# Six weight subtractions on another engine, dt's rows in another buffer, and a scheduler that estimates matmuls and a shared port differently, in a two-layer recurrent decoder step

## The chip, the cores and the metric

One Trainium2 chip, one of its cores. The metric is the device time of one execution in microseconds. Engines as the profile names them: PE (matrix products), PEld (its weight loads), DVE and ACT (elementwise work, both can read PSUM), POOL (elementwise work on SBUF alone here), SP (issues most DMAs).

## What is computed

One step of a two-layer decoder trunk, for a prompt of 512 tokens and 8 samples of one token (520 columns in all), width 1024, all in float32.

```python
# layer 0
u = rmsnorm(h, norm_w) @ w_in
a_x, a_gate, b_z, b_xbc, b_dt = split(u)
a_xc = causal_conv(a_x, s_ac, a_conv_w, a_conv_b)
a_y, new_ah = rg_lru(a_xc, s_ah, a_w_r, a_b_r, a_w_i, a_b_i, a_lam)
a_out = a_y * silu(a_gate)
xbc = silu(causal_conv(b_xbc, s_bc, b_conv_w, b_conv_b))
dt = softplus(b_dt + b_dt_bias)
y, new_bs = ssd_scan(bx, dt, -exp(b_a_log), bb, bcm, s_bs)     # cumulative sums of dt * a by chunk
b_out = group_norm((y + b_d * bx) * silu(b_z)) * b_norm_w
h = h + concat(a_out, b_out) @ w_out
h = h + sigmoid(h @ ple_g) * (p @ ple_w)
# layer 1
q, fx, v, gate = split(rmsnorm(h, norm_w) @ w_in)
o, new_c = hgrn2_scan(q, k, v, g, s_c)                          # 16 heads, k and g from fx
h = h + (head_norm(o) * c_norm_w * silu(gate)) @ w_out
h = h + sigmoid(h @ ple_g) * (p @ ple_w)
# end
y = rmsnorm(h, norm_f)
```

## The kernel before

Every large matrix product is a block of 128 output features over all 520 columns, as two halves of 260. Products run in a reduced 32-bit form (fp32r), so a weight tile wraw that a 1 MB DMA brings is split into whi (a cast) and wlo (wraw - whi, a subtraction), and the tokens into xh and xl; a block of 1024 inputs is 3 x 8 x 2 = 48 matmuls: hi x hi, lo x hi, hi x lo. The splits are most of the work of DVE and ACT.

The stages follow each other on PE. First the transposes of the tokens and the embedding product pl of layer 0 (weights wraw7 and pp, evacuated through the tile htmp and stored to DRAM as pl_d). Then layer 0's projections: ax0 to ax7 (the RG-LRU branch; tokens normed to n and sqt, split to xnh and xnl; the first two blocks' weights are called wax), the gates g (weights gw, inputs xg), xbc (through the tile bcs; POOL keeps a copy of its sample columns in LCb), the SSD chunks (yd, with the decay matrix built in wsl), the gate and z projections, the output projection, the embedding gate. Layer 1 begins with pl of its own (evacuated by plt, stored to pl_d) while its norm is formed (n1b, acc1, n, xh), then f, q, v and g of 16 heads in pairs, with the small products A, kt, kv, o and ot of each head among them. The tail is the last norm.

dt's chain: dt_project (L1168) multiplies the tokens by dtws into two PSUM banks, copies them to a tile dth, and transposes dth into the bank dtT; DVE adds the bias, ACT takes exp, log1p_of (L920) on POOL evaluates a series of some twenty instructions on the tile dtt, and PE multiplies dtt by a triangle into acs, the cumulative sums that every SSD chunk needs.

dth has the tag "misc", and that tag has one buffer. The raw embedding input, each xg0 to xg7, and two tiles of the LRU's and the samples' outputs have the same tag. They take the buffer in the order in which the program names them.

What sets the order of the work. Helpers (tt, stt, ts, copy, ...) do not issue anything; they record operations (L269) with a priority, the place in the main stream of matrix products, shifted by the `side` that surrounds them. Plan.order (L348) then runs a list schedule over the engines with an estimate of every instruction: an engine that comes free takes the ready operation with the earliest priority. urgency (L336) puts what the main stream waits for ahead by MARGIN, unless its side is pinned. issue (L494) emits everything in this order, at one line of the file, L510. So all engines' queues are decided by the estimates. The estimate of a 260-column matmul is 260 columns at 2.4 per ns and 0.003 us on top (0.111 us), and double where the clock is thought halved. No estimate has DVE and POOL in each other's way.

```python
c = c + 0.003 * len(calls) if cols[int(t / 3.41333) - 1] >= 3060 else 2.0 * c
...
dth = new("cst", [2 * NH, D], "misc", "dth")
```

split_unit(u, hi, lo, eng) at L627 splits one weight tile: the cast on ACT or DVE (the planner's choice), the subtraction on eng.

Of the kernel before, what the change touches and what calls it, by code (L numbers as in the profile page):

```python
# [11 lines left out]
F32 = mybir.dt.float32  # L12
# [7 lines left out]
PSUM = bass.MemoryType.PSUM  # L20
# [7 lines left out]
D = 1024  # L28
# [11 lines left out]
SYNC = 0.12  # L40
PATIENCE = 3.26
ROW = 1 << 24
# how far ahead of a unit its weights are split and loaded, in us of the main stream
SPLIT_AHEAD, LOAD_AHEAD = 1.67, 11.54
# how far ahead of the main stream goes what it waits for, in us
MARGIN = 38.78
# an engine waits for an instruction that is more urgent by URGENT us, up to this part of the time of the one at hand
# [32 lines left out]
def _mm(n, a, k):  # L80
    out, m = k["out"] if "out" in k else a[0], k["lhsT"].shape[-1]
    if m < 128 and out.off >= 32 * ROW:
        # beside the one before it, in other columns of the array
        return 65 if k["rhs"].dtype == F32R else 125
    return max(n, 256) if k["rhs"].dtype == F32R else 4 * max(n, m)
# [16 lines left out]

class Buf:
    """A tile that is allocated when its first instruction is issued."""
# [7 lines left out]
class View:  # L112
    """A view of a Buf; offset and strides are in elements, a partition is ROW apart."""
# [86 lines left out]
class Op:  # L200
    """One instruction, in a form for each engine that may take it, or a few matrix products that stay together."""
# [8 lines left out]
class Plan:  # L210
    """Instructions are collected first and then put in an order: with an estimate of what each of them costs, an
    engine that comes free takes the instruction of the earliest place in the program whose operands are there."""
# [6 lines left out]
    # -- collecting --  # L219
# [23 lines left out]
    def side(self, start=0.0, rate=0.0, pinned=False):  # L243
        """Instructions whose place is moved, by a start and by their own time so far; pinned: for good."""
# [6 lines left out]
    def together(self, *views):  # L251
        """Instructions that wait until all of some operands are written."""
# [5 lines left out]
    def block(self, main=False):  # L258
        """Matrix products that stay together."""
# [66 lines left out]
    # -- ordering --  # L326
    def hold_banks(self):
        """A PSUM bank is taken only when what its readers wait for otherwise is already on its way."""
# [7 lines left out]
    def urgency(self):  # L336
        """What an instruction of the main stream waits for is put ahead of it."""
# [10 lines left out]
    def order(self):  # L348
# [13 lines left out]
        bus, cols, lanes = 0.0, defaultdict(float), defaultdict(list)  # L362
# [30 lines left out]
        def pick(e, t):  # L393
            """The instruction for engine e at time t, or when there may be one."""
# [7 lines left out]
            while av:  # L402
# [13 lines left out]
                if func and table not in IN_SET[func]:  # L416
                    # another table: first what the loaded one can do, for a while
# [14 lines left out]
            if got:  # L432
                heapq.heappush(av, got)
                hold = {"dve": HOLD_DVE, "act": HOLD_ACT, "pool": HOLD_POOL}.get(e)
                if hold:
                    # rather wait a little for one that is more urgent than be in its way
# [8 lines left out]
        while left:  # L445
# [27 lines left out]
            else:  # L473
                if e == "pe":
                    # the clock is halved after a window with too few columns
                    c = c + 0.003 * len(calls) if cols[int(t / 3.41333) - 1] >= 3060 else 2.0 * c
                    cols[int((t + c) / 3.41333)] += op.cols
                elif func and table not in IN_SET[func]:
                    table = IN_SET[func][0]
                    c += 1.29  # L480
                fin = clk[e] = t + c
# [11 lines left out]
    # -- issuing --  # L493
# [27 lines left out]
# the place of the side work: its start after the instructions it follows, and its pace  # L521
# [9 lines left out]
def hybrid_decode_step_kernel(ctx: ExitStack, tc: tile.TileContext, I, O, mode="both"):  # L531
# [31 lines left out]
    def grab(name):  # L563
        """One of four PSUM banks for the side work; it is given back by its last reader."""
# [26 lines left out]
    def copy(out, in_):  # L591
        """A copy on either engine."""
        plans[-1].record(("act", "copy", (out, in_), {}), ("dve", "tensor_copy", (out, in_), {}))

    def scaled(out, in_, s):
        """in_ times a column, on either engine."""
# [85 lines left out]
    def project_both(tiles, pair, kmap):  # L682
        """One or two tiles of 128 output features (column block m of unit u) over all tokens."""
# [28 lines left out]
    def split_p(pk, ps8, pp, layer):  # L712
        """p with features on partitions, in two float32r parts."""
# [49 lines left out]
    # the tensor engine's clock rises only under load: products of constants until the first tokens are there  # L763
# [43 lines left out]
    def rsqrt_mean(dst, src, n, width):  # L807
        """(src / n + eps) ** -0.5 on a few columns."""
# [8 lines left out]
    def scale_split(src, w, R, xh, xl, name):  # L817
        """src times its weight and a row of factors per token, in two float32r parts."""
# [6 lines left out]
    # the tokens with features on partitions; they come back as the residual  # L825
# [94 lines left out]
    def log1p_of(z, n, lo):  # L920
        """log(1+z) for z in [0,1], from the odd series in z/(2+z)."""
# [14 lines left out]
    def accurate_exp(t, k):  # L936
        """exp in place: the table on x/2^k, where it is exact to float32, and k squarings."""
# [4 lines left out]
    def buffers():  # L942
        """Samples: convolution buffers and LRU state with features on partitions."""
# [11 lines left out]
    def tables():  # L955
        pool.memset(triu, 1.0)
        select(triu, [[1, 128]], 0, -1, 0.0)
        # RG-LRU: -8 softplus(-lam), halved for the sigmoid from tanh
# [1145 lines left out]
```

## Time and profile before

| what | us |
|---|---|
| three runs | 1078.21, 1078.10, 1075.42 (median 1078.1) |
| span of the profiled execution (first to last instruction) | 1075.0 |
| PE busy | 1044.0 |
| DVE busy | 778.2 |
| ACT busy | 509.1 |
| POOL busy | 144.6 |

The profile records one more execution; its span is what lies between its first and its last instruction. A row of the timeline gives start and duration in us, engine, line, operation, the tile written and the tiles read, and in brackets how long the engine sat idle ahead of it and for whom. As every recorded operation is issued at L510, lines don't tell the stages apart; tiles do. Matmul rows may join several matmuls (x4).

### The profile page before, as it was taken

The page shows a single profiled execution, that of the slowest core. Times are in us where ns is not written, and L with a number is a line of the kernel's source. Part 1 is how long each engine was busy: PE and PEld are TensorE (multiplying, and loading weights), DVE is VectorE, ACT ScalarE, POOL GpSimd, SP SyncE. Part 2 cuts the span into 40 slices and gives each one's busy share as a digit, 9 for nine tenths or more (in the row PEclk, how much of TensorE's full clock was granted, in tenths as well). Part 3 has the DMA queues.
Part 4 walks back from the last instruction along what each step waited for, and adds up shares of the span by engine and source line. Part 5 has one row for each costly group of instructions (what it writes and reads, how often), then busy time and mean ns, then how long its engine had stood idle before and what let it go on. Part 6 is the DMA issues. An engine that isn't in the chain of part 4 may idle for free.

```text
span 1075.0 us, 21235 instructions
## 1 busy us (share of the span) xinstructions
PE 1044.0 (97%) x8595; PEld 1023.0 (95%) x8595; DVE 778.2 (72%) x1521; ACT 509.1 (47%) x1196; POOL 144.6 (13%) x247
## 2 busy tenths in 40 slices
PE   9899989999999999999999999999999999999995
PEld 8899988899999999999999999999999999999995
DVE  6879988999997546774858576675765757667753
ACT  6476648636464212353445545333463344642453
POOL 3755475200000000100000000000000000000000
PEclk9899999999999999999999999999999999999998
DMA  8603226444686233563433433253342433335311
GB/s 275 244 21 99 80 51 206 147 142 140 200 249 210 79 115 131 162 208 88 135 108 115 128 102 111 90 155 91 115 124 87 143 98 112 97 89 199 119 40 44
DMA packets 130466, 138.43 MB, mean 129 GB/s; under 512 B 13704, under 2 KB 111128, under 8 KB 130344
## 3 DMA queue, kind: packets, MB, share of 16 engines
q1 hardware_dynamic: 130136, 136.93, 41.0%
q8 instruction: 69, 1.13, 0.4%
q14 instruction: 37, 0.30, 0.1%
q0 software_dynamic: 224, 0.06, 0.0%
HBM read 111.71 MB, written 25.44 MB: 128 GB/s over the span
## 4 chain that ended last, share of the span: by engine, by line
PE 84%; POOL 5%; DVE 4%; DMA 3%; ACT 2%; issue 1%; POOLq 0%; ACTq 0%; DVEq 0%
PE o L510 11%; PE g L510 10%; PE f L510 9%; PE v L510 9%; PE q L510 9%; PE pg L510 7%; PE ag L510 4%; PE ob L510 4%; PE z L510 4%; PE oa L510 3%; PE ax L510 3%; PE xbc L510 1%; POOL csm L510 1%; PE A L510 1%; PE kv L510 1%
## 5 line engine op out<-in xcount | busy, mean ns | idle before, releaser
L510 DVE TENSOR_TENSOR wlo<-wraw,whi 128x1024 fp32r<-128x1024 f32 (+1 forms) x143 | 173.4, 1213 | 3.2 <-ACT whi L510 1.8
L510 ACT CAST whi<-wraw 128x1024 fp32r<-128x1024 f32 (+1 forms) x63 | 65.2, 1036 | 126.3 <-PE q L510 41.2
L510 POOL TENSOR_TENSOR at__1873<-at__1873,nhalf 128x4 f32<-128x4 f32 (+1 forms) x24 | 20.8, 866 | 501.1 <-DVE at__1873 L510 501.1
L510 DVE CAST whi<-wraw 128x1024 fp32r<-128x1024 f32 x80 | 55.3, 692 | 36.7 <-PE v L510 11.9
L510 PE MATMUL g<-xh,whi 128*128 128x260 f32 x256 | 55.8, 299 | 0.0
L510 PE MATMUL q<-xh,whi 128*128 128x260 f32 x256 | 53.2, 289 | 0.0
L510 PE MATMUL o<-oh,whi 128*128 128x260 f32 x256 | 52.6, 286 | 0.0
L510 PE MATMUL v<-xh,whi 128*128 128x260 f32 x256 | 52.1, 285 | 0.0
L510 PE MATMUL v<-xh,wlo 128*128 128x260 f32 x256 | 51.5, 283 | 0.0
L510 PE MATMUL g<-xl,whi 128*128 128x260 f32 x256 | 51.5, 283 | 0.0
L510 PE MATMUL o<-oh,wlo 128*128 128x260 f32 x256 | 51.5, 283 | 0.0
L510 PE MATMUL g<-xh,wlo 128*128 128x260 f32 x256 | 51.5, 283 | 0.0
L510 PE MATMUL o<-ol,whi 128*128 128x260 f32 x256 | 51.4, 282 | 0.0
L510 PE MATMUL q<-xl,whi 128*128 128x260 f32 x256 | 51.4, 282 | 0.0
L510 PE MATMUL v<-xl,whi 128*128 128x260 f32 x256 | 51.4, 282 | 0.0
L510 PE MATMUL q<-xh,wlo 128*128 128x260 f32 x256 | 51.4, 282 | 0.0
L510 PE MATMUL f<-xh,whi 128*128 128x260 f32 x240 | 50.6, 292 | 0.0
L510 PE MATMUL f<-xl,whi 128*128 128x260 f32 x240 | 48.2, 282 | 0.0
L510 PE MATMUL f<-xh,wlo 128*128 128x260 f32 x240 | 48.2, 282 | 0.0
L510 DVE SCALAR_TENSOR_TENSOR l1a<-q,lbt,l1a 128x260 f32<-128x260 f32 (+1 forms) x32 | 14.0, 479 | 44.1 <-PE q L510 44.0
L510 DVE SCALAR_TENSOR_TENSOR l1c<-l1d,l1c 128x128 f32<-128x128 f32 x128 | 40.9, 345 | 0.6 <-ACT l1c L510 0.6
L510 PEld LDWEIGHTS o<-oh,whi 128*128 128x128 f32 x256 | 39.3, 189 | 0.9 <-issue 0.8
(507 smaller groups left out, 3362.2 us busy)
## 6 DMA issues: line engine op xcount, KB each, us to landing
wraw<-in_c_w_in_dram SPq DMA_DIRECT2D x32, 1024.0 KB
wraw<-in_ab_w_in_dram SPq DMA_DIRECT2D x15, 1024.0 KB
wraw<-in_ab_w_out_dram SPq DMA_DIRECT2D x8, 1024.0 KB
wraw<-in_ple_gate_dram SPq DMA_DIRECT2D x8, 1024.0 KB
l1c<-in_state_c_dram SPq DMA_DIRECT2D x16, 512.0 KB
out_dram<-l1c SPq DMA_DIRECT2D x16, 512.0 KB
wraw<-in_c_w_out_dram SPq DMA_DIRECT2D x8, 1024.0 KB
pl<-pl_d SPq DMA_DIRECT2D x2, 2080.0 KB
```

Of the source, the lines that this page charges most:

```text
L510: getattr(f, name)(*a, **k)
```

## The change

Six subtractions move from POOL to DVE: the one of the embedding's weights (1024 columns), the one of ax1's weights (1024), and the four of the gates' weights gw (512 each), whose side becomes pinned. dth becomes a stretch of htmp, a tile with room of its own there. The planner's estimate of a matmul gains 0.0115 us in place of 0.003 (0.120 us for 260 columns), and a new function says which instructions of DVE and POOL use a port that they share; the planned start of such an instruction is put behind the planned end of the other engine's last one. Comments and docstrings are gone, so lines have moved by some 20.

```diff
+MM_GAP = 0.0115
...
+def shares_port(e, name, a, k):
+    ap = [v for v in list(a) + list(k.values()) if _is_ap(v)]
+    if name == "memset":
+        return False
+    if e == "pool":
+        return True
+    if name in ("tensor_copy", "tensor_scalar"):
+        return all(v.space != PSUM for v in ap)
+    out = k["out"] if "out" in k else a[0]
+    return sum(v.space != PSUM and v is not out and _free(v) > 1 for v in ap) > 1
...
-        bus, cols, lanes = 0.0, defaultdict(float), defaultdict(list)
+        bus, cols, lanes, port = 0.0, defaultdict(float), defaultdict(list), {"dve": 0.0, "pool": 0.0}
...
-                    c = c + 0.003 * len(calls) if cols[int(t / 3.41333) - 1] >= 3060 else 2.0 * c
+                    c = c + MM_GAP * len(calls) if cols[int(t / 3.41333) - 1] >= 3060 else 2.0 * c
...
+                if e in port and shares_port(e, *calls[0]):
+                    t = max(t, port["pool" if e == "dve" else "dve"])
+                    port[e] = t + c
                 fin = clk[e] = t + c
...
-        split_unit(sec["proj0b"], pp0[:, 2080:3104], pp0[:, 3104:4128], pool)
+        split_unit(sec["proj0b"], pp0[:, 2080:3104], pp0[:, 3104:4128])
-            split_unit(sec["ax"] + i, wax[:, i * 2048:i * 2048 + 1024], wax[:, i * 2048 + 1024:i * 2048 + 2048],
-                       pool if i else dve)
+            split_unit(sec["ax"] + i, wax[:, i * 2048:i * 2048 + 1024], wax[:, i * 2048 + 1024:i * 2048 + 2048])
...
-    with side(GW_LATE):
+    with side(GW_LATE, pinned=True):
...
-                tt(gw[:, 1, a, k:k + 4], wg[:, a, k:k + 4], gw[:, 0, a, k:k + 4].bitcast(F32), SUB, pool)
+                tt(gw[:, 1, a, k:k + 4], wg[:, a, k:k + 4], gw[:, 0, a, k:k + 4].bitcast(F32), SUB)
...
-        dth = new("cst", [2 * NH, D], "misc", "dth")
+        dth = htmp[:2 * NH, 1888:1888 + N]
```

What this does to the queues is seen in three places. The first is the start. On DVE, from the last products of the norm to dt's weights, before:

```order
L510 SCALAR_TENSOR_TENSOR n0_6_451<-xT_199,pt_301,acc1_215 128x520
L510 SCALAR_TENSOR_TENSOR sqt_147<-xT_199,pt_301,acc1_215 128x520
L510 TENSOR_TENSOR xnl_360<-sqt_147,xnh_338 128x520
L510 CAST whi2_484<-wraw2_335 128x1024
L510 TENSOR_TENSOR xnl_360<-n0_6_451,xnh_338 128x520
L510 TENSOR_TENSOR xnl_360<-sqt_147,xnh_338 128x520
L510 TENSOR_TENSOR wlo2_519<-wraw2_335,whi2_484 128x1024
L510 TENSOR_TENSOR wlo3_530<-wraw2_335,whi3_494 128x1024
L510 TENSOR_TENSOR dtws_511<-htmp_85,dtws_511 128x8x16
```

and after:

```order
L529 SCALAR_TENSOR_TENSOR n0_6_477<-xT_202,pt_315,acc1_199 128x520
L529 SCALAR_TENSOR_TENSOR sqt_147<-xT_202,pt_315,acc1_199 128x520
L529 TENSOR_TENSOR xnl_359<-n0_6_477,xnh_340 128x520
L529 TENSOR_TENSOR xnl_359<-sqt_147,xnh_340 128x520
L529 TENSOR_TENSOR wlo2_517<-wraw2_317,whi2_430 128x1024
L529 TENSOR_TENSOR wlo3_533<-wraw2_317,whi3_453 128x1024
L529 TENSOR_TENSOR gw_409<-bcs_260,gw_409 128x512 x4
L529 TENSOR_TENSOR dtws_494<-htmp_85,dtws_494 128x8x16
```

The cast of whi2 (weights of ax2, in the load wraw2) has left DVE and the four subtractions of gw stand ahead of dtws. That cast is on ACT now. ACT before, in the same stretch (htmp<-pl are the copies that empty the embedding's PSUM):

```order
L510 COPY htmp_85<-pl05_350 128x520
L510 CAST wax_280<-wraw1_322 128x1024
L510 CAST xnh_338<-sqt_147 128x520
L510 CAST gw_413<-bcs_268 128x512 x4
L510 COPY htmp_85<-scT_432 128x480
L510 CAST xnh_338<-sqt_147 128x520
L510 COPY htmp_85<-pl07_390 128x520
L510 CAST xnh_338<-n0_6_451 128x520
```

and after:

```order
L529 COPY htmp_85<-pl05_352 128x520
L529 CAST wax_278<-wraw1_291 128x1024
L529 CAST gw_409<-bcs_260 128x512 x2
L529 CAST whi2_430<-wraw2_317 128x1024
L529 COPY htmp_85<-pl06_374 128x520
L529 COPY htmp_85<-pl07_393 128x520
L529 CAST whi3_453<-wraw2_317 128x1024
L529 CAST gw_409<-bcs_260 128x512 x2
```

The copies of pl06 and pl07 stand behind the cast of whi2, and so behind the load wraw2; before, DVE had pl06's. The second place is dt's transposes on PE, before, among the products of xbc2:

```order
L510 MATMUL xbc2_1610<-xnh_338,whi15_1503 128x260 x2
L510 MATMUL xbc2_1610<-xnl_360,whi15_1503 128x260 x2
L510 MATMUL xbc2_1610<-xnh_338,wlo15_1522 128x260 x2
L510 MATMUL dtT_1632<-ident_77,dth_1617 128x32 x5
L510 MATMUL xbc2_1610<-xnh_338,whi15_1503 128x260 x2
```

and after, among those of ax7:

```order
L529 MATMUL ax7_1178<-xnh_340,whi7_1084 128x260 x2
L529 MATMUL ax7_1178<-xnl_359,whi7_1084 128x260 x2
L529 MATMUL ax7_1178<-xnh_340,wlo7_1099 128x260 x2
L529 MATMUL dtT_1190<-ident_77,htmp_85 128x32 x5
L529 MATMUL ax7_1178<-xnh_340,whi7_1084 128x260 x2
```

dtT stood behind 878 matmuls and stands behind 596; acs stood behind 1021, inside xbc5, and stands behind 955, inside xbc3. POOL's queue up to the end of dt's chain (htmp and dtt are the chain; LCb, xa, ahs and csm are the samples'), before:

```order
L510 COPY LCb<-bcs 128x11
L510 TENSOR_SCALAR htmp<-htmp 128x80
L510 TENSOR_TENSOR csm<-LCb,pt 128x32
L510 TENSOR_TENSOR htmp<-htmp 128x80
...
L510 TENSOR_SCALAR htmp<-htmp 128x80
L510 TENSOR_TENSOR dtt<-dtt,htmp 128x80
L510 TENSOR_TENSOR xa<-xa,lg 128x8
L510 TENSOR_TENSOR dtt<-dtt,hb 128x80
```

and after:

```order
L529 COPY LCb<-bcs 128x11
L529 TENSOR_SCALAR htmp<-htmp 128x80
L529 TENSOR_TENSOR htmp<-htmp 128x80
...
L529 TENSOR_TENSOR xa<-xa,lg 128x8
L529 TENSOR_SCALAR htmp<-htmp 128x80
L529 TENSOR_TENSOR htmp<-htmp 128x80
L529 COPY ahs<-xa 128x9
L529 TENSOR_SCALAR htmp<-htmp 128x80
L529 TENSOR_TENSOR dtt<-dtt,htmp 128x80
L529 COPY LCb<-bcs 128x11
L529 TENSOR_TENSOR dtt<-dtt,hb 128x80
```

From dtt's first row to its last the queue has 28 rows before and 41 after, with the copies LCb of xbc0, xbc1 and xbc2 between them, since xbc comes later than dt now. The third place is ACT at the start of layer 1, where the last blocks of pl are emptied, before:

```order
L510 COPY plt_5371<-pl_5434 128x520
L510 COPY acc_215<-n1b 128x416
L510 COPY plt_5371<-pl_5456 128x520
L510 CAST xh_5500<-n_0_5482 128x520
L510 CAST xh_5500<-sqt 128x520
```

and after:

```order
L529 COPY plt_5370<-pl_5433 128x520
L529 COPY plt_5370<-pl_5455 128x520
L529 COPY acc_199<-n1b 128x416
L529 CAST xh_5499<-n_0_5490 128x520
L529 COPY plt_5370<-pl_5481 128x520
```

The copy of the norm's factors (acc, from n1b) has gone behind one more copy of pl.

## The prediction

> **What bounds the kernel now.** I read the page first, then TensorE's waits, then the engines in stretches, and last the single instructions around each wait.
>
> ```profile
> span 1075.0 us, 21235 instructions
> PE 1044.0 (97%) x8595; PEld 1023.0 (95%) x8595; DVE 778.2 (72%) x1521; ACT 509.1 (47%) x1196; POOL 144.6 (13%) x247
> ```
> ```profile
> 20.00:40.00 20.00, 16.06 (x113) 15.03 (x112) 19.19 (x21) 11.81 (x22) 9.62 (x10) 0.89 0.60 182
> 220.00:300.00 80.00, 80.00 (x672) 78.41 (x671) 75.17 (x148) 39.91 (x149) 1.55 (x1) 1.00 0.57 176
> 460.00:1000.00 540.00, 539.87 (x4496) 532.66 (x4497) 367.73 (x805) 242.36 (x572) 20.77 (x24) 1.00 0.39 117
> ```
> Columns: length, then busy time (and count) of PE, PEld, DVE, ACT, POOL, then the granted clock. TensorE bounds the kernel. From 460 to 1000 us nothing is to be had: 539.87 of 540 us, 4496 matmuls, so **0.120 us each**; that is my price of a matmul. What an order can win lies ahead of 460. DVE, 72% over the span, is nearly full at 20 to 40 (19.19 of 20) and at 220 to 300 (75.17 of 80), so in layer 0 added DVE work can become a TensorE wait.
>
> ```profile
> PE acs L510 <- POOL dtt L510: 4.2, 1, 4.2
> PE pl L510 <- ACT plt L510: 2.2, 1, 2.2
> PE ax L510 <- ACT htmp L510: 2.1, 1, 2.1
> PE g L510 <- DVE xg L510: 2.0, 1, 2.0
> ```
> Each row gives what PE waited for, the sum in us, the times and the longest. acs on dtt is dt's chain, ax on htmp the start, g on xg the first gates, pl on plt the start of layer 1; no other wait is longer than 2 us. Two cost more than their length, because the clock falls behind them:
>
> ```profile
> 32.20:35.60 3.40, 1.35 (x9) 0.92 (x8) 3.40 (x3) 0.43 (x1) 3.40 (x3) 0.99 0.05 0
> 35.60:39.00 3.40, 2.66 (x12) 2.66 (x13) 3.40 (x5) 2.79 (x5) 0.80 (x2) 0.50 0.54 196
> 39.00:42.40 3.40, 3.40 (x18) 3.40 (x18) 3.40 (x5) 0.71 (x5) 2.99 (x4) 0.50 1.07 382
> 141.40:144.80 3.40, 1.57 (x14) 1.35 (x12) 1.92 (x3) 0.54 (x1) 3.10 (x7) 1.00 0.44 130
> 144.80:148.20 3.40, 1.03 (x9) 1.03 (x10) 0.04 (x1) 0.30 (x2) 2.87 (x10) 1.00 0.00 0
> 148.20:151.60 3.40, 3.40 (x18) 3.22 (x17) 3.40 (x6) 2.64 (x9) 1.89 (x4) 0.50 0.04 10
> ```
> After a stretch of 3.4 us in which PE is busy for 1.35 (40%) or 1.03 (30%), the next runs at 0.50; after 1.57 (46%) it doesn't. A half-clock stretch costs 3.4 x 0.5 = 1.7 us. Two are paid near 36 to 42 us and one at 148.
>
> **1. The six subtractions.** They are on POOL before, on DVE after.
>
> ```profile
> 17.57 2.38 POOL L510 TENSOR_TENSOR pp<-wraw,pp 128x1024 fp32r<-128x1024 f32 x1
> 27.37 2.38 POOL L510 TENSOR_TENSOR wax<-wraw,wax 128x1024 fp32r<-128x1024 f32 x1 [7.43 <-ACT wax L510]
> ...
> 29.79 6.46 POOL L510 TENSOR_TENSOR gw<-bcs,gw 128x512 fp32r<-128x512 f32 x4
> ```
> ```profile
> 19.81 1.22 DVE L510 TENSOR_TENSOR wax<-wraw,wax 128x1024 fp32r<-128x1024 f32 x1
> ...
> 22.96 0.69 DVE L510 TENSOR_TENSOR xnl<-n,xnh 128x520 fp32r<-128x520 f32 x1
> ...
> 27.64 2.40 DVE L510 CAST xnh<-n 128x520 fp32r<-128x520 f32 x1
> 29.97 1.78 DVE L510 TENSOR_TENSOR xnl<-sqt,xnh 128x520 fp32r<-128x520 f32 x1
> ...
> 35.06 1.76 DVE L510 SCALAR_TENSOR_TENSOR n<-xT,pt,acc 128x520 f32<-128x520 f32 x1
> ```
> On DVE they cost 2 x 1.22 + 4 x 0.69 = 5.2 us, where POOL takes 11.2. While POOL runs the last five of them DVE's own rows stretch: from 27.64 to 35.06 five rows, 2.40 and four of about 1.77, 9.5 us, where they would take some 0.7 each, 3.6. That is 5.9 us lost on DVE, as much as the subtractions cost it. So DVE comes out level, and the stretch in which ax waits is gone.
>
> ```profile
> 27.78 0.39 PE L510 MATMUL ax<-xnh,wax 128*128 128x260 f32 x1 [0.61 <-DVE htmp L510]
> ```
> ```profile
> 47.05 0.40 PE L510 MATMUL dt<-xnh,dtws 128*32 128x260 f32 x2
> ```
> Before, ax0 and ax1 (96 matmuls, 11.5 us at 0.120) take from 27.78 to 47.05: 19.3 us. After, they start later. ACT's cast of whi2 stands ahead of the last two copies htmp<-pl that free ax0's and ax1's PSUM, and it waits for the 1 MB load wraw2. Before, the loads of this time end near 29.5:
>
> ```profile
> GB/s 0 8 101 384 380 255 364 393 403 357 418 318 338 308 355 408 318 172 291 312 317 109 21 149 203 367 379 381 394 236 0 0 0 0 0 7 67 190 404 408
> ```
> (1 us a number.) wraw1 is issued earlier after the change; I estimate the landing at 28 to 28.6, then the cast, which this row has for wax1, and the copy:
>
> ```profile
> 26.25 1.05 ACT L510 CAST wax<-wraw 128x1024 fp32r<-128x1024 f32 x1 [1.33 <-DMA wraw<-in_ab_w_in_dram]
> ```
> With 28.3 + 1.05 + 0.6 for a copy of 128x520 (the plt row below has 0.59) + 0.2 to reach PE, ax0 begins at about 30.2, some 3.2 us after PE's work runs out at 27. Then nothing holds it: DVE's list from 20.0 us, at 0.67 for a product and 0.61 for a subtraction, ends the last xnl at 34.9, gw at 39.9 and dtws at 40.2, each ahead of its matmul. dt starts at 30.2 + 11.5 = 41.7 with the full clock. A wait of 3.2 us leaves some stretch of 3.4 with under 40% busy unless both share it evenly, about 3 phases in 4, so I take one half-clock stretch: 43.4, a **gain of 3.6**. Bounds: 5.3 with none, 1.9 with two. By the Trainium skill, TensorE: Matmul & The Clock Gate, section What's actually happening, the clock falls after a whole idle window of some 3.4 us; a 3.2 us wait would then cost no clock and the gain would be 5.3. This trace halves it after stretches 30 and 40% busy, against that rule, and the trace decides.
>
> g's wait (2.0) I leave as it is: xg stands behind lbt on DVE, which waits for POOL's lbt products in both orders. Bounds: 0.4 to 2.4.
>
> **2. dth in htmp, dt's chain earlier.** dtT moves from matmul 878 to 596 of the built order, acs from 1021 to 955. POOL's first and last instruction of dt's chain before:
>
> ```profile
> 127.97 0.84 POOL L510 TENSOR_SCALAR dtt<-dtt 128x80 f32<-128x80 f32 x1 [3.35 <-DVE dtt L510]
> ...
> 146.76 0.35 POOL L510 TENSOR_TENSOR dtt<-dtt,hb 128x80 f32<-128x80 f32 x1
> ```
> POOL's chain takes 19.1 us and PE waits 4.2 at its end. After: acs is due 66 matmuls (7.9 us) earlier, from 142.9 to 135, less the gain at the start: about 131. dtT itself is due near 90 - 3.6 = 86; DVE reads it where its list allows, near 96. POOL's chain is now 41 rows with the samples' among them; at 0.65 each, from 0.35 alone and 0.84 beside a busy DVE, 27 us, so 124. One thing holds it longer: POOL's queue has the copies LCb of xbc1 and xbc2 inside the chain. xbc1 ends 84 matmuls (10.1 us) ahead of acs; after it come DVE's copy (0.7), LCb (0.5), twelve of the chain (7.8), LCb of xbc2 and the last (1.1): 10.1 us. So it ends as PE arrives. I take a wait of 0.4 (between 0 and 2), which halves no clock: **gain 4.2 - 0.4 + 1.7 = 5.5**.
>
> **3. The rest of the new order.** At layer 1's start ACT before copies acc1 and then waits:
>
> ```profile
> 455.59 0.51 ACT L510 COPY acc<-n1b 128x416 f32<-128x416 f32 x1 [1.10 <-PE n1b L510]
> 459.48 0.59 ACT L510 COPY plt<-pl 128x520 f32<-128x520 f32 x1 [3.38 <-DMA pl_d<-plt]
> ```
> After, the plt copy stands first; the norm's acc1, and so n, xh and f0 behind it, wait for that DMA too. xh starts after acc1's copy (0.51) and the product n on DVE, so f0 is **1.0 later** (0 to 2.7, with a half-clock stretch).
>
> In layer 0 the order is new and DVE as full as it was, so a wait like g's on xg (2.0) may come up elsewhere: none to two of them, I take one, **2.0 lost**.
>
> Layer 1's transposes ot of five even heads move up to before kt, some 1.1 us nearer to their input:
>
> ```profile
> 511.18 0.68 DVE L510 TENSOR_TENSOR l1a<-o,at__1873 128x512 f32<-128x512 f32 x1
> ```
> ```profile
> 512.75 0.60 PE L510 MATMUL ot<-ident,l1a 128*128 128x128 f32 x4
> ```
> The input ends at 511.86 and the matmul starts at 512.75, 0.9 later: moved by 1.1 it waits 0.2. I take 0 (up to 3.5 for five at 0.7). The tail is the same chain; nothing. The planner's new numbers issue nothing themselves.
>
> **Sum:** -3.6 - 5.5 + 1.0 + 2.0 = -6.1 us on a span of 1075.0. The runs lie 0.4 to 3.2 above that span; against their median, 1078.1 - 6.1 = **1072.0**.
>
> **Rivals.** (A) DVE becomes the bound in layer 0: 19.19 of 20 and 75.17 of 80 speak for it. Then what PE gains ahead of 140 us comes back as waits for wsl or xg before 300: only some 1 us is left, 1077. (B) dt's chain is late all the same: three LCb copies and the samples' work interleave, DVE streams beside it. At 0.84 for each of the twelve in the last stretch, POOL ends 12 x 0.19 = 2.3 us later, PE waits 2.7 and the clock halves once: 4.0 of the 5.5 are lost, 1076.0. The Trainium skill, SBUF — State Buffer, section Who interferes with whom, speaks for it: a DVE instruction with two SBUF inputs contends with a GpSimd instruction that reads SBUF, and subtractions on DVE are of this kind. The rows agree in size, 0.35 alone against 0.84, but they don't show the full block on every row that it states. (C) whi2's wait for wraw2 costs more than the subtractions gain: at a landing of 29.5, as before, ax0 starts at 31.3 with two slow stretches, gain 0.8 instead of 3.6: 1074.8. (D) The clock holds over the start's wait, as it did after the stretch that was 46% busy: 1.7 less, 1070.3. (E) **Slower:** in layer 1 a truer matmul time takes the estimate's slack (0.111 before, 0.120 measured) out of the order: what the planner placed 7% early now stands just in time. If real latencies (the POOL power beside DVE above all) exceed its estimates by 0.7 us, each of 16 heads waits at ot: 11.2, so 1078.1 - 6.1 + 11.2 = 1083.2. It decides from about 0.4 us a head. For it: a 0.9 us margin less 1.1. Against it: only five heads move so.
>
> **Chances.** Forecast 0.44, D 0.15, A 0.11, B 0.10, C 0.08, E 0.12. Faster by over 0.3% (3.2 us, about what a measurement tells from no change) means under 1074.9: most of the forecast and D, half of C: 0.62. Same: A, B, the rest of C and the forecast's edge: 0.25. Slower, over 1081.3: E and a sum of bad bounds: 0.13. The best bounds together (5.3, g 1.6, acs 5.9, no new waits) give 1065; the range goes from there to 1081, which leaves out most of E.
>
> **What would show it.** Right: no wait acs on dtt over 2 us and full clock behind it; one stretch near 30 at half clock or none; dt's first matmul at 42 to 44; DVE rows near 0.69 between 27 and 36. Wrong: the chain of dtt ending after PE's xbc3 begins to idle; a new wait for wsl, xg or bcs between 60 and 300 over 3 us; PE below 539 of 540 between 460 and 1000, with waits at ot or kv; f0 over 3 us later than the gain before it allows.

## The result, and the profile after

The changed kernel takes 1089.5 us (median of four runs, 1088.2 to 1096.1) where the kernel before takes 1078.0 beside it: ratio **1.0141, 95% interval 1.0118 to 1.0163**. The forecast was 1072.0, with a range of 1065 to 1081: wrong in sign and out of the range. The profiled run has a span of 1088.8, 13.8 over the span before. First the page of the changed kernel, engines by busy time:

```profile
span 1088.8 us, 21249 instructions
PE 1046.1 (96%) x8595; PEld 1022.0 (94%) x8595; DVE 788.8 (72%) x1579; ACT 494.6 (45%) x1144; POOL 138.6 (13%) x241
```

PE executes the same 8595 matmuls and is busy 2.1 us longer; the other 11.7 are waits. TensorE's waits, with the sum, the times and the longest in us:

```profile
PE ax L529 <- ACT htmp L529: 10.8, 2, 10.3
PE yd L529 <- DVE wsl L529: 3.1, 3, 2.7
PE acs L529 <- POOL dtt L529: 2.8, 1, 2.8
PE oa L529 <- DVE aol L529: 2.8, 1, 2.8
PE pl L529 <- ACT plt L529: 2.0, 1, 2.0
...
PE g L529 <- DVE xg L529: 1.8, 2, 1.2
```

The wait of ax on htmp has gone from 2.1 to 10.8, acs from 4.2 to 2.8, and oa, which waited 0.4, waits 2.8. The stretches of the changed kernel that answer to those shown of before (length, busy time of PE, PEld, DVE, ACT, POOL, granted clock, DMA share, GB/s):

```profile
20.00:40.00 20.00, 9.19 (x64) 8.63 (x63) 10.58 (x17) 8.80 (x15) 2.31 (x5) 0.71 0.63 189
300.00:320.00 20.00, 17.00 (x127) 16.55 (x126) 18.62 (x42) 13.31 (x47) 0.00 (x0) 0.91 0.67 217
460.00:1000.00 540.00, 536.85 (x4449) 527.40 (x4449) 372.67 (x843) 230.76 (x532) 29.08 (x25) 1.00 0.40 120
28.80:32.20 3.40, 0.00 (x0) 0.00 (x0) 3.40 (x7) 1.05 (x1) 0.00 (x0) 0.50 0.19 57
32.20:35.60 3.40, 0.00 (x0) 0.00 (x0) 0.43 (x1) 0.00 (x0) 0.00 (x0) 0.50 0.16 41
35.60:39.00 3.40, 2.11 (x8) 1.81 (x9) 0.00 (x0) 1.67 (x3) 0.00 (x0) 0.50 0.81 304
```

From 20 to 40 PE works 9.19 of 20 us, where it worked 16.06. From 460 to 1000, where nothing was to be had and I had put the loss at 0, it executes 4449 matmuls instead of 4496. Landmarks on PE, from each tile's own rows (starts of matmuls, in us):

| | before | after | difference |
|---|---|---|---|
| ax, first matmul | 27.8 | 36.4 | +8.6 |
| dt, first matmul | 47.1 | 51.0 | +3.9 |
| acs, first matmul (66 matmuls earlier in the list) | 147.2 | 140.7 | -6.5 |
| ag, last matmul | 279.3 | 284.2 | +4.9 |
| oa, last matmul | 351.7 | 360.8 | +9.1 |
| f of layer 1, first matmul | 461.7 | 471.3 | +9.6 |
| q of layer 1, first matmul | 485.0 | 495.5 | +10.5 |
| o of layer 1, last matmul | 1009.0 | 1021.7 | +12.7 |
| last transpose ft | 1064.5 | 1078.5 | +14.0 |

So the time is lost in six places: the start up to dt (3.9), the way to ag (1.0), oa (4.2), the way to layer 1's f (0.5), layer 1 (3.1) and the tail (1.3).

**The start** is read in three views. SP's queue in the changed kernel (start, us, what is issued):

```profile
22.81 0.38 SPq L529 DMA_DIRECT2D wraw<-in_ab_w_in_dram  x1
23.23 0.85 SPq L529 DMA_DIRECT2D dcol<-in_b_d_dram  x1
24.18 0.97 SPq L529 DMA_DIRECT2D pl_d<-htmp  x1
25.19 1.36 SPq L529 DMA_DIRECT2D dcol<-in_b_d_dram  x1
26.65 2.00 SPq L529 DMA_DIRECT2D pl_d<-htmp  x1
```

its ACT and PE (in brackets the idle time before the row and what ended it):

```profile
30.90 1.05 ACT L529 CAST whi<-wraw 128x1024 fp32r<-128x1024 f32 x1 [3.68 <-DMA wraw<-in_ab_w_in_dram]
35.72 0.59 ACT L529 COPY htmp<-pl 128x520 f32<-128x520 f32 x1 [3.77 <-DMA pl_d<-htmp]
37.92 0.59 ACT L529 COPY htmp<-pl 128x520 f32<-128x520 f32 x1 [1.61 <-DMA pl_d<-htmp]
```
```profile
36.36 0.80 PE L529 MATMUL ax<-xnh,wax 128*128 128x260 f32 x2 [10.28 <-ACT htmp L529]
```

and one step of the chain of waits, of the changed kernel and of the kernel before:

```profile
26.65 11.19 DMA pl_d<-htmp
```
```profile
22.45 4.48 DMA pl_d<-htmp
```

The two loads of dcol (64x8 single elements, 2 KB each) now stand ahead of two stores pl_d<-htmp; before, both stood behind those two (stores at 22.45 and 23.55, dcol from 24.46). The store behind both loads takes 11.19 us from issue to landing, where a store of the same 260 KB took 4.48; the one issued at 24.18, behind the first load, lands just ahead of 35.72. The copies that empty ax0's and ax1's PSUM write into htmp, and each waits for one of these two stores. PE idles over two stretches and works at half clock up to 42.0.

### The profile page after: what moved, and what is told of

It reads as the page before. It is cut to its first block, busy times and chain, and to the rows that moved or that the text cites. A ratio compares the mean times of both kernels' runs of the same rounds, so it can differ in the third digit from the quotient of the medians.

```text
span 1088.8 us, 21249 instructions
## 1 busy us (share of the span) xinstructions
PE 1046.1 (96%) x8595; PEld 1022.0 (94%) x8595; DVE 788.8 (72%) x1579; ACT 494.6 (45%) x1144; POOL 138.6 (13%) x241
## 4 chain that ended last, share of the span: by engine, by line
PE 67%; DVE 14%; DMA 7%; ACT 5%; POOL 4%; issue 2%; SPq 0%; ACTq 0%; DVEq 0%; POOLq 0%
PE o L529 10%; PE f L529 9%; PE v L529 8%; PE q L529 8%; PE g L529 8%; PE pg L529 7%; PE ob L529 4%; DVE wlo L529 3%; PE oa L529 2%; PE ax L529 2%; DVE smp L529 2%; DVE bx L529 2%; PE kv L529 1%; POOL htmp L529 1%; PE A L529 1%
## 5 line engine op out<-in xcount | busy, mean ns | idle before, releaser
L529 ACT CAST whi<-wraw 128x1024 fp32r<-128x1024 f32 (+1 forms) x67 | 69.4, 1036 | 140.6 <-PE q L529 54.2
L529 POOL TENSOR_TENSOR at__1786<-at__1786,nhalf 128x4 f32<-128x4 f32 (+1 forms) x24 | 27.6, 1151 | 495.1 <-DVE at__1786 L529 495.1
L529 DVE CAST whi<-wraw 128x1024 fp32r<-128x1024 f32 x76 | 52.4, 690 | 21.1 <-PE pg L529 6.7
L529 DVE SCALAR_TENSOR_TENSOR l1c<-l1d,l1c 128x128 f32<-128x128 f32 x128 | 42.6, 346 | 0.2 <-ACT l1c L529 0.2
L529 ACT ACTIVATE l1c<-l1c,l1d 128x128 f32<-128x128 f32 x106 | 32.7, 390 | 20.8 <-DMA l1d<-vsd 20.8
```

The lines of the kernel that those rows point to most:

```text
L529: getattr(f, name)(*a, **k)
```

## Experiments

A ratio here is to the kernel before on the same chip, with its 95% interval. Where an order is edited, an instruction is moved in the finished list of one queue (of DVE, ACT and POOL in the run that reads dtT early) and all other queues keep theirs.

**1. dcol's place.** In the changed kernel SP issues dcol behind the last store x_d; in the kernel before SP issues it ahead of the third and the fourth store pl_d<-htmp.

```diff
+def moved(seq):
+    d = _find(seq, "sp", "dcol", None)
+    if d:
+        s = [x for x in seq if _io(x)[0] == "sp" and _io(x)[1] == "x_d"]
+        seq = _move(seq, d, s[-1])
+    return seq
...
-        for op in self.order():
+        for op in moved(self.order()):
```

> The changed kernel with one edit: SP issues the two loads dcol (2 KB each, in 4-byte pieces) behind the stores x_d, where before they stand ahead of the stores pl_d; every other queue is as it was. Theory 1 (the small loads hold up what SP issues behind them for some 10 us; so the stores pl_d land late, so ACT's copies htmp<-pl and with them ax0 wait until 36.4): ax0 starts at 31 to 33, dt at 45 to 47 in place of 51.0, the time falls by 4 to 6 us, to about 1084. Theory 2 (rival C of the prediction: it is the cast of whi2, ahead of the copies, and its load): no change, ax0 stays at 36, within 1 us of 1089.5.

> The kernel before with one edit: SP issues the two loads dcol one ahead of the third and one ahead of the fourth store pl_d, as the changed kernel has them; every other queue is as it was. Theory 1 (the small loads): DVE's copy htmp<-pl at 27.0 and ACT's after it wait until about 35, ax0 starts at 34 to 36 in place of 27.8, dt at 49 to 51 in place of 47.05, the time rises by 2 to 4 us, to 1080 to 1082. Theory 2 (whi2's cast and its load): no change, 1078.

dcol late: 1084.2 us, ratio 1.0087 (1.0068 to 1.0107) in place of 1.0141. Its ACT and PE:

```profile
28.89 1.04 ACT L555 CAST whi<-wraw 128x1024 fp32r<-128x1024 f32 x1 [2.25 <-DMA wraw<-in_ab_w_in_dram]
29.84 1.11 ACT L555 COPY htmp<-pl 128x520 f32<-128x520 f32 x2
```
```profile
30.48 0.80 PE L555 MATMUL ax<-xnh,wax 128*128 128x260 f32 x2 [4.44 <-ACT htmp L555]
```

The copies follow the cast at once, ax starts at 30.5 (36.4) and dt at 44.0 (51.0). That is close to the start as I had forecast it: ax0 at 30.2, dt at 43.4.

dcol early in the kernel before: ratio 1.0021 (1.0006 to 1.0035). The wait is there, on DVE, which has that copy in this kernel (at 27.03 without the edit):

```profile
31.01 0.70 DVE L537 COPY htmp<-pl 128x520 f32<-128x520 f32 x1 [5.24 <-DMA pl_d<-htmp]
```

ax starts at 31.8, 4.0 later. But dt comes at 46.7, 0.4 earlier than without the edit and not at the 49 to 51 expected: the later waits of ax (0.5 and 0.7 for xnl, 2.1 for htmp) are gone, so the start absorbs the whole delay. f's first matmul is where it was (461.7), so the 0.2% doesn't come from the start. In this profile a half-clock stretch over f's first matmuls (460.9 to 464.3), which the profile of the kernel before doesn't have, costs some 1.3 us; where the rest comes from was not found. What the same two loads cost depends on whether anything else is late.

**2. Two waits in layer 0 of the changed kernel.** DVE does the 13 products of the samples ahead of aoh and aol after them; and, in another run, DVE reads dtT at once and POOL's chain starts earlier.

```diff
+    w = [x for x in seq if _io(x)[0] == "dve" and _io(x)[1] in ("aoh", "aol")]
+    if w:
+        i = seq.index(w[0])
+        sm = [x for x in seq[:i] if _io(x)[0] == "dve" and _io(x)[1] == "smp"][-13:]
+        for x in reversed(sm):
+            seq = _drop(seq, x, w[-1])
```
```diff
+    r = _find(seq, "dve", "dtt", "dtT")
+    if r:
+        at = _find(seq, "pe", "dtT", None)[-1]
+        for x in r:
+            seq = _go(seq, x, at)
+            at = x
...
```

> The changed kernel with one edit: on DVE the last 13 products of the samples' state (smp) ahead of the casts aoh and the subtractions aol stand behind them, with the store that follows them; all else as it was. Theory 3 (DVE's list is the bound at 300 to 320; PE's wait of 2.8 for aol and the half-clock stretch behind it are the price of these 13, about 3.6 us of DVE): the wait is under 0.5, no half clock at 312, 3.5 to 4.5 us less, 1085.5. Rival (DVE is full there in any order, the samples' products come late in turn and the group norm bn waits for them): the wait moves to bn, less than 1 us gained.

> The changed kernel with one edit: DVE reads dtT as soon as PE has made it (93 us in place of 113), ACT's exp follows, POOL's chain begins ahead of the sample product that waits for DVE until 113.3 and its second half ends ahead of the copies LCb of xbc1 and xbc2; all else as it was (one activation table load is placed earlier). Theory 5 (the wait of 2.8 at acs is the late start of the chain on DVE, not the chain's length): chain from 107 to 130, no wait at acs, no half clock at 144, 4 to 4.5 us less, 1085. Rival (POOL's instructions beside DVE are the limit, and what is put behind the chain on POOL makes DVE wait for its samples): the wait at acs goes but DVE idles for POOL, and g or xbc wait: less than 1.5 us gained.

DVE of the changed kernel at that place:

```profile
308.02 2.19 DVE L529 SCALAR_TENSOR_TENSOR smp<-smp,xd 128x128 f32<-128x128 f32 x8
310.12 0.76 DVE L529 CAST aoh<-xa 128x520 fp32r<-128x520 f32 x2
310.80 4.96 DVE L529 TENSOR_TENSOR aol<-xa,aoh 128x520 fp32r<-128x520 f32 x8
315.68 0.69 DVE L529 SCALAR_TENSOR_TENSOR zs<-zs,z 128x520 f32<-128x520 f32 x1
```

With aol ahead of the products the ratio is 1.0143 (1.0126 to 1.0160), no better. The wait has moved to the row behind aol:

```profile
PE oa L608 <- DVE zs L608: 2.3, 1, 2.3
```

DVE is full here (18.62 of 20 us above), so what is put first makes something else late: the rival of that run. With dt read early the ratio is 1.0176 (1.0151 to 1.0201): the wait of acs is gone, and others take its place:

```profile
PE ah L623 <- DVE bx L623: 3.8, 1, 3.8
PE g L623 <- DVE xg L623: 2.7, 3, 1.6
...
PE acsT L623 <- ACT at__1786 L623: 1.9, 1, 1.9
```

**3. Each part of the change alone, in the kernel before.** The edits are those of the diff: the subtractions, dth in htmp, the matmul time, the port.

```diff
-                tt(gw[:, 1, a, k:k + 4], wg[:, a, k:k + 4], gw[:, 0, a, k:k + 4].bitcast(F32), SUB, pool)
+                tt(gw[:, 1, a, k:k + 4], wg[:, a, k:k + 4], gw[:, 0, a, k:k + 4].bitcast(F32), SUB)
```
```diff
-        dth = new("cst", [2 * NH, D], "misc", "dth")
+        dth = htmp[:2 * NH, 1888:1888 + N]
```
```diff
-                    c = c + 0.003 * len(calls) if cols[int(t / 3.41333) - 1] >= 3060 else 2.0 * c
+                    c = c + MM_GAP * len(calls) if cols[int(t / 3.41333) - 1] >= 3060 else 2.0 * c
```
```diff
+                if e in port and shares_port(e, *calls[0]):
+                    t = max(t, port["pool" if e == "dve" else "dve"])
+                    port[e] = t + c
```

> The kernel before with the six subtractions on DVE (and gw's products kept there), none of the other three parts; on SP's queue dcol stands ahead of the x_d stores, two stores pl_d<-htmp after wraw. Theory 1 (the start lost its gain to dcol, not to the subtractions): here dt's first matmul comes at 43 to 45 instead of 47.1, DVE's rows between 27 and 36 are near 0.7, and if acs still waits some 4 on dtt the time is 2 to 4 us under the kernel before, ratio 0.997. Rival (the subtractions on DVE cost the start as much as they give): dt at 47 or later, ratio 1.000 or more, and DVE the engine that PE waits for ahead of 47. Layer 1's end minus its start within 0.7 us of before by theory 1, since the loss there is put down to the matmul time; the rival that any new order loses there gives 2 to 3 more.

> The kernel before with dt's product in htmp alone: dtT stands 135 instructions of PE's list earlier, acs 33 earlier. As I predicted: acs waits under 2, no half clock behind it, 5.5 us less, ratio 0.995. Rival (the chain is late all the same because DVE reads dtT late, as in the changed kernel at 113): acs waits 2.5 to 5 and a stretch near it runs at half clock, within 2 us of before, ratio 0.999 to 1.001. The start, the order of dcol and layer 1 as before in both.

> The kernel before with the estimate's truer matmul time alone (0.0115 in place of 0.003). Theory (the matmul time takes slack out of the order, my rival E, in small pieces): PE loses 2 to 3 us between layer 1's start and its end and 1 to 2 in the tail, without a listed wait over 1; ratio 1.002 to 1.005. Rival (layer 1's loss has to do with the port's estimate or is any new order's): layer 1 within 0.7 us of before; then the ratio is within 0.002 of 1 but for new waits in layer 0.

> The kernel before with the estimate's port of DVE and GpSimd alone: SP's queue has dcol ahead of the third and fourth store pl_d<-htmp, as in the changed kernel. Theory 1 (dcol holds the stores): the copies htmp<-pl come 4 us or more later than in before, ax's first matmul at 31 or later, with a wait for htmp of 4 to 10; the start gains nothing, dt at 46 to 50. acs stands 36 places later, so its wait is under 1 instead of 4.2. Sum between -3 and +6 us. Rival (dcol costs only where the subtractions are on DVE): ax first as in before at 27.8. If layer 1 and the tail lose here 2 to 3 and 1 to 2 us, they are the port's; if not, the matmul time's.

Measured: subtractions 1.0081 (1.0055 to 1.0107), dth 1.0030 (1.0016 to 1.0044), matmul time **1.0240** (1.0209 to 1.0272), port 1.0012 (1.0000 to 1.0025). None is a gain, and each expectation missed one of its numbers at least. The subtractions do gain at the start (ax's last matmul starts 2.2 us earlier). The new order puts dt's product 36 us later, yet dtT is written 15 us earlier (110.7 instead of 126.2) and POOL's chain begins at 112.5 instead of 128.0. But the chain now takes 29.5 us where it took 19.1, and acs stands 60 matmuls earlier. The stretch around acs:

```profile
140.00:150.00 10.00, 7.91 (x43) 7.73 (x44) 5.04 (x10) 2.82 (x8) 6.76 (x8) 0.59 0.08 19
```

acs waits 6.7 there, and the clock is halved for most of these 10 us. dth alone: dtT is written at 93.0, DVE reads it at 122.9, and acs still waits 4.7, as the rival had it. The matmul time alone brings the longest waits of all:

```profile
PE ax L511 <- DVE htmp L511: 7.6, 1, 7.6
PE acs L511 <- POOL dtt L511: 7.6, 1, 7.6
PE ah L511 <- POOL ahs L511: 4.0, 1, 4.0
```

and here too dcol has moved ahead of one more store on SP (it goes out at 23.56, that store at 27.50), and the copy htmp<-pl at 38.69 has waited 3.1 for pl_d. I had looked for its loss in layer 1 (2 to 3 us; it is 3.7 there, 1.5 in the tail) and not for the 21 us ahead of it. The port alone leaves layer 1 as it was. It too has dcol among the stores (one load ahead of the fourth), and ACT's copy at 31.72 has waited 3.5 for pl_d; but ax0 had its PSUM by then and starts at 27.7, not at 31, and dt comes at 44.2, 2.9 earlier than before.

**4. The matmul time in layer 1.** The estimate takes one matmul time for layer 0's instructions and the other for layer 1's: in the changed kernel the old one for layer 1, without and with dcol late; in the kernel before the new one for layer 1.

```diff
-                    c = c + MM_GAP * len(calls) if cols[int(t / 3.41333) - 1] >= 3060 else 2.0 * c
+                    c = c + (0.003 if op.i >= getattr(self, "mark", 1 << 30) else MM_GAP) * len(calls) if cols[int(t / 3.41333) - 1] >= 3060 else 2.0 * c
...
+    plans[-1].mark = len(plans[-1].ops)
     layer1_fast()
```

> The changed kernel whose estimate takes the old matmul time (0.003) for layer 1's instructions and the new one for layer 0's: layer 0's order is the changed kernel's on every engine, layer 1's heads stand as before. Theory (the truer matmul time costs layer 1 and the tail their slack): f's first matmul as in the changed kernel at 471.3, layer 1 (f's first to o's last) 547.2 to 547.6 instead of 550.3, kv 13.0 and o's 128-column products 24.3 in sum instead of 14.0 and 25.0, the tail 0 to 1.5 shorter: 3 to 4.5 us less than the changed kernel, ratio to the kernel before 1.010 to 1.011. Rival (layer 1's loss is one of drift, from where layer 0 leaves the buffers): layer 1 still 550, ratio 1.014.

> The kernel before with the new matmul time for layer 1's instructions alone: layer 0 in the order of before. The theory's mirror: to f's first matmul as before (461.7), layer 1 550 to 551 instead of 547.2, the tail 0 to 1.5 longer: 3 to 5 us more, ratio 1.003 to 1.0045; the hidden waits of 0.2 stand ahead of kv and ot. Rival (the loss needs the changed layer 0): 1.000.

> Both repairs, dcol behind the x_d stores and the old matmul time for layer 1. If the two losses add: start as with dcol late (ax first 30.5, dt first 44.0), layer 1 547.2 to 547.6, so 3 to 4.5 us under dcol late alone (1084.2, ratio 1.0087), ratio 1.0045 to 1.006; the profile near the kernel before. What is left over 1 is then layer 0's waits (acs, oa) and half clocks. Rival (they overlap): ratio 1.008 or more.

Old time in layer 1 of the changed kernel: 1.0084 (1.0055 to 1.0112). New time in layer 1 of the kernel before: 1.0052 (1.0031 to 1.0072). Both repairs: **1.0017 (0.9997 to 1.0037)**; the two losses add, within their intervals. Layer 1, from f's first matmul to o's last pair, sorts all sixteen profiles by this number alone:

| matmul time of layer 1's order | kernel: length in us |
|---|---|
| old | before 547.2, with dcol early 548.2, dth alone 548.6, subtractions alone 547.5, port alone 547.3, port with dcol late 547.3, changed with old time in layer 1 547.6, with both repairs 548.2, without the new time 547.5, without dth too 548.2 |
| new | changed 550.3, with dcol late 551.0, with aol first 550.4, with dtT read early 550.5, matmul time alone 550.9, before with new time in layer 1 551.9 |

Part of the spread within a line is a half-clock stretch that reaches over f's first matmuls: some 1.6 us of dth alone's 548.6 and 0.8 of the 551.9.

TensorE's own list of waits doesn't show these 3 to 4 us, since a wait this short lies under the end of the matmul before it. The list of its weight loads does, for the kernel before with the new time in layer 1 and its tail:

```profile
PEld kv L510 <- ACT l1b L510: 1.6, 8, 0.5
PEld ft L510 <- ACT h L510: 1.3, 3, 0.8
PEld ot L510 <- DVE l1a L510: 1.2, 5, 0.2
PEld os L510 <- DVE l1d L510: 0.7, 2, 0.5
```

The kernel before has one wait on these four tiles:

```profile
PEld ft L510 <- DVE h L510: 0.7, 1, 0.7
```

The changed kernel has kv (1.5), ft (1.2) and os (0.5) in that list; with the old time in layer 1 they are gone. The starts show the same. PE of the kernel before with the new time in layer 1, at one head's ot:

```profile
535.57 0.41 PE L510 MATMUL v<-xh,wlo 128*128 128x260 f32 x2
536.01 0.66 PE L510 MATMUL ot<-ident,l1a 128*128 128x128 f32 x4
```

Its DVE:

```profile
535.26 0.69 DVE L510 TENSOR_TENSOR l1a<-o,at__1873 128x512 f32<-128x512 f32 x1 [0.76 <-POOL at__1873 L510]
```

and the kernel before:

```profile
512.51 0.40 PE L510 MATMUL g<-xh,wlo 128*128 128x260 f32 x2
512.75 0.60 PE L510 MATMUL ot<-ident,l1a 128*128 128x128 f32 x4
```

A pair of matmuls takes 0.24 from start to start; here ot comes 0.44 after the pair ahead of it, so it waits 0.20, for the product l1a that ends at 535.95. Five heads in this run wait so at ot. Summed by tile, the starts share out the 4.7 us: kv 2.2, f 1.7 (0.8 of it the half clock), ot 1.2 and os 0.6 more than before, and o 0.9 less.

**5. The port's order with dcol late.** The kernel before with the port's estimate, and dcol behind the x_d stores.

> The kernel before with the port's estimate (1.0012), and dcol moved behind the x_d stores on SP. By theory 1 the copy htmp<-pl no longer waits 3.5 for a store, ax loses its waits of 2.3 and 1.0 on htmp, dt's first matmul comes at 42 to 43 instead of 44.2: 1 to 3 us less, ratio 0.9985 to 1.0003, perhaps ahead of the kernel before. Rival (as in the kernel before with dcol moved, the start absorbs it: ax waits for xnh or xnl later instead): dt at 44 or later, ratio 1.0012.

1074.9 us, ratio **0.9980 (0.9963 to 0.9996)**: the copy htmp<-pl doesn't wait any more, dt starts at 42.6, and the kernel is a little ahead of both.

**6. The matmul time taken out everywhere.** The changed kernel with its estimate's old matmul time, all else as changed; and the same without dth in htmp, which is the kernel before with the subtractions and the port.

```diff
-                    c = c + MM_GAP * len(calls) if cols[int(t / 3.41333) - 1] >= 3060 else 2.0 * c
+                    c = c + 0.003 * len(calls) if cols[int(t / 3.41333) - 1] >= 3060 else 2.0 * c
```

> The changed kernel with the old matmul time in the whole estimate: the subtractions, dth in htmp and the port stay. On SP's queue dcol then stands behind four stores pl_d<-htmp by the planner's own choice. Theory (the new matmul time brought every loss: dcol's place, layer 1's hidden waits, and through layer 0's order acs and oa): layer 1 at 547.2 to 547.6, dt at 42 to 44.5, no ax wait over 4, oa's 48.5 us as in before, and with dt's chain read at once acs's wait under 3: ratio 0.995 to 1.000. Rival (the subtractions and dth lose in layer 0 by themselves, as each does alone in the kernel before, 1.0081 and 1.003): ratio 1.003 to 1.010, with acs waiting 4 or more and a half clock behind it.

> The kernel before with the subtractions on DVE and the port's estimate, without dth in htmp and without the new matmul time. If dt's product in htmp is what makes acs late, acs waits less here than with it; if the subtractions are (alone they gave 6.7 at acs), it waits 4 or more and the ratio is 1.003 or more. dt at 42 to 44.5, layer 1 at 547.2 to 547.6 in both.

Changed kernel without the matmul time: **1071.5 us, ratio 0.9955 (0.9938 to 0.9971)**. Without dth too: **1068.0 us, 0.9932 (0.9916 to 0.9947)**, the fastest kernel here. No list was moved by hand in either. (dt stands behind more matmuls in these lists and starts near 80, so its landmark, expected at 42 to 44.5, says nothing; ax's last matmul starts at 90.0 and 87.9 instead of 95.4. In the first, DVE reads dtT at 112.5, though it is written at 93.4, so that chain isn't read at once either.) The first kernel's stretch and the second's:

```profile
460.00:1000.00 540.00, 540.00 (x4502) 532.80 (x4501) 371.65 (x810) 235.14 (x561) 23.78 (x24) 1.00 0.39 117
```
```profile
20.00:40.00 20.00, 19.50 (x163) 19.11 (x161) 17.63 (x26) 14.80 (x31) 6.67 (x11) 1.00 0.64 175
300.00:320.00 20.00, 19.96 (x167) 19.75 (x166) 18.20 (x37) 15.07 (x54) 1.24 (x1) 1.00 0.73 235
```

Layer 1 is full again, and the start and oa of the faster kernel have no half clock and no wait of more than 0.7 us. acs waits 1.8 and 3.0 in the two; of the two answers that I had set down for the second kernel neither holds: acs waits more without dth, and the kernel is faster all the same.

## Why the prediction was wrong, point by point

The forecast was -6.1 us; the trace says +13.8. Its steps, in its order, beside the changed kernel and three of the runs (starts of matmuls in the profiles; differences to the kernel before, in us):

| | forecast | changed | dcol late | both repairs | no matmul time |
|---|---|---|---|---|---|
| dt's first matmul | -3.6 | +3.9 | -3.1 | -2.8 | (stands elsewhere) |
| ag's last matmul | -8.1 with one wait lost half way | +4.9 | -4.5 | -4.4 | -7.2 |
| oa's last matmul | -7.1 | +9.1 | -1.5 | -1.6 | -6.9 |
| o's last matmul in layer 1 | -6.1 | +12.7 | +2.7 | +0.1 | -4.6 |
| last transpose ft | -6.1 | +14.0 | +4.8 | +0.5 | -4.1 |

(The forecast's column adds its terms in their order: 3.6, 5.5, then 2.0 of new waits, half by ag and the other half by oa, and 1.0 at f0.)

- **1, the start (forecast -3.6, measured +3.9): the failed step is "I estimate the landing at 28 to 28.6, then the cast, which this row has for wax1, and the copy".** It priced the copies by the load wraw2 alone. They have a second condition, the store that empties htmp, and on SP's queue that store had been put behind dcol. I looked at the queue's loads and not at the stores. The cast itself is also late, at 30.90. With dcol late the step holds nearly to the number: cast at 28.89 (forecast 28 to 28.6), ax 30.5 (30.2), dt 44.0 (43.4), with two half-clock stretches, the first mostly idle, where I had one. DVE's rows do shrink to 0.69, so the subtractions' own sum was right.
- **2, dt's chain (forecast -5.5, measured about -1.4): the failed step is "DVE reads it where its list allows, near 96".** No row stood behind that number. DVE reads it at 113:

```profile
113.31 0.22 DVE L529 TENSOR_TENSOR dtt<-dtT,hb 128x80 f32<-128x80 f32 x1
...
114.06 0.23 DVE L529 TENSOR_TENSOR dtt<-dtT,dtt 128x80 f32<-128x80 f32 x1
```

though dtT is written at 93.6. POOL's chain then takes 26.2 us (114.4 to 140.6; I had said 27) and acs waits 2.8 with a half-clock stretch, as before: 1.4 is left of 5.5. The start isn't to blame, since with dcol late acs waits 2.8 as well. Rival B had a wait of 2.7 and the half clock, for another reason. Reading dtT earlier is no cure (experiment 2).
- **3, the new order in layer 0 (forecast one wait, +2.0).** At oa alone it is +4.2: 2.8 for aol instead of 0.4, and half clock from 311.7 to 315.1. Moving DVE's work there moves the wait, so this is rival A's mechanism, a full DVE, in a place that I didn't name.
- **3, f0 (forecast +1.0):** from oa's last matmul to f's first +0.5, within the bounds of 0 to 2.7.
- **3, layer 1 and the tail (forecast 0, measured +3.1 and +1.3).** The failed step is "moved by 1.1 it waits 0.2. I take 0". The 0.2 is what ot measures, in the runs where ot is late; in the changed kernel itself it is kv and, less, os that are. This is rival E with its sign, at other tiles of the same heads, and with 3.1 of its 11.2 us. By my own condition (0.4 us a head) it would not have decided; it only added.
- **"The planner's new numbers issue nothing themselves."** True, and the costliest sentence. In this combination of four parts the matmul time made all of the loss: 1.0141 with it, 0.9955 without it. It acts in three pieces that add, within their intervals: dcol's place (1.0141 to 1.0087), layer 1 and the tail (1.0141 to 1.0084; both 1.0017), and the rest of layer 0's order (1.0017 to 0.9955). With it out, the other three parts bring 4.8 us by the ratio, where my sum said 6.1. That the sum comes near for that kernel is in part luck: up to ax's last matmul it gains some 5 us instead of 3.6, and acs' wait falls by 2.4 where the sum had 3.8.

Of the signs that I had named, dt's first matmul at 51 (42 to 44 was right) and PE below 539 of 540 between 460 and 1000 (536.85) point to two of the three places that cost most; oa, at 4.2 us, is the third.

**Open.** Why a matmul time that is nearer to the measured 0.120 us gives a worse order is argued, not shown: the planner's other numbers (its lead times and due dates) were there while the estimate ran 7% fast, and that surplus covered latencies which it doesn't model, such as a 2 KB load, for which it books 0.02 us of the bus and 1.65 us of fixed times. For layer 1 the waits of the weight loads bear this out. For layer 0's remaining 0.6% I have only the whole. The tail's 1.3 us come and go with the same number: from o's last matmul to the last ft it takes 56.7 to 58.0 us with the new time and 54.6 to 56.2 with the old one. There the last transposes ft wait for ACT's h (1.2 us in the changed kernel's list of weight loads); why ACT has it later was not found. Whether lead times set anew for the new matmul time would turn the loss round wasn't tried.

## What to carry to other kernels

When an estimate that orders the work is corrected, price the order and not the correction: list, for every wait that you expect to shorten, all conditions of the instruction that ends it, the stores and the small loads on the same DMA queue among them. A truer number in one place of a planner can cost more than a real gain beside it; test it by itself, and by stage, as each part alone can mislead (three parts that lose or tie alone gain 0.45% together). Waits that are too short for TensorE's own list show in the list of its weight loads, and in start-to-start times.

## What the runs showed of the hardware

- A load of 2 KB in single elements is not short. With dcol late, the chain of waits has one of its loads:

```profile
36.33 7.77 DMA dcol<-in_b_d_dram
```

7.77 us from issue to landing, among x_d's stores; and a 260 KB store issued behind such loads lands late. Over all runs, a store for which a copy htmp<-pl waited took 4.4 to 4.9 us from issue to landing with no dcol load ahead of it (7.7 in a fourth run), 8.3 to 11.5 with one ahead, and 11.1 to 12.5 with both. By the Trainium skill, DMA: Bandwidth & Descriptors, section Queues, rings and completion order, each DMA engine takes the descriptors of one queue in the order of its ring; the runs agree, since moving the two loads behind the stores, with nothing else changed, gave back 0.0054 of the 0.0141 by which the ratio stood over 1.
- The clock changes in steps of 3.41 us. In the sixteen profiles, from 16 us on up to the last transposes, a full-clock stretch in which PE was busy under 45% of the time was always followed by half clock, and one over 52% never; between the two it went both ways. At half clock a stretch busy up to 80% was followed by another at half clock, and one over 85% by the full clock. That is why one wait can cost two such stretches, as at 35.6 to 42.4 in the kernel before.
- DVE and POOL: in the kernel before, from 29.97 to 35.06, four rows of DVE beside POOL's gw start 1.70 us apart, and POOL's four take 6.46 us, 1.6 each. This fits one of the two working at a time; no run here tests it.
